# Two-layer hybrid backbone on one core: where the up stage's operands lie, when T3 and T4 are made, and which banks and loads the down stage uses

## Chip, core and metric

One core of one Trainium2 chip runs the whole program. The metric is the device time of one execution in microseconds (us). Engines: TensorE (PE, its weight loads PEld), VectorE (DVE), ScalarE (ACT), GpSimd (POOL), SyncE (SP, here only a queue of DMA issues). Each engine runs its instructions in a fixed order and stops at the first one whose inputs are not there.

## What is computed

A backbone of two layers (DEPTH 2) over 1024 latent tokens and 256 context tokens of width 1024, float32. Cut to what the change touches:

```python
for i in range(2):
    mod_lat = silu(c) @ ada_w[i] + ada_b[i]          # adaLN: shift, scale, gate, twice; six parts of 1024
    mod_ctx = silu(c_ctx) @ ada_w[i] + ada_b[i]
    ...                                               # attention, Hyena, linear attention, output projection
    h_lat = h_lat + g2_l * swiglu(modulate(rms_norm(h_lat, norm2_g), sh2_l, sc2_l), w1, w3, w2)
    if i == 0: h_ctx = h_ctx + g2_c * swiglu(...)     # the context only in the first layer
swiglu(u) = (silu(u @ w1) * (u @ w3)) @ w2            # hidden width 2816 = 22 column blocks of 128
```

## The kernel before

**Products.** A float32 matrix is kept as a rounded high part and a remainder; `split` makes them (ACT casts the high part, POOL subtracts it to get the low part, line 187), and `mm3` multiplies two such operands with three matmuls. A matmul over 512 columns is the unit of work. Weights stand as the stationary operand, tokens as the moving one.

**Up stage** (`up`). Latent tokens are two blocks of 512 (blocks 0 and 1), the context block 2 has 256. Weight column blocks are taken in pairs (p, p+1). Over a pair and the two token blocks the kernel does a block product in Strassen's manner with seven products instead of eight: sums of weight quarters (S1 to S4, DVE, line 1716) against sums of token blocks (T1 to T4, with B11, B21, B22 as the blocks themselves). `norm_sums` is a generator that makes the token sums of block 1 while TensorE works: T1, then B22 and T2, then T3 and T4 (`difference`, lines 1602 and 1603: two DVE subtractions or additions and one on POOL for each quarter, then a cast and a POOL subtraction). Three pairs 0, 2, 4 have their first products (`first`) ahead, while the sums are made; eight whole pairs 6 to 20 follow, and pairs 0, 2, 4 are finished last. In layer 0 `context_tokens()` also normalizes the context block (tile u2, lines 399, 401, 405) before the whole pairs. The split weights go to tiles `hl` (a fixed region) or `hs` (its own tiles, cycled by `ring`). Gated results are written to device memory (`g_d`) by ACT's queue.

**Down stage** (lines 1500 to 1570). For each pair of hidden blocks, `load(j)` brings a block of w2 (`raw`) and of the gated values (`graw`, all 1280 tokens, 1024 in layer 1), splits both into high and low parts (`w2s`, which lies in `hl` or in a tile w2/w; `gs`, tiles g), and TensorE computes 24 outputs (8 output blocks by three token blocks) in turn in the six banks of role 0, (6,7,0,1,2,3). Banks 4 and 5 are role 1. DVE adds each output to the residual h (line 1561), which has to be loaded back from `h_d` in 24 loads (16 in layer 1) at the stage's start.

**adaLN work.** The modulation vectors are computed between the rest of the work, in items of half a part: `ada_dve` has DVE accumulate 8 loaded weight slices (`nsq`, lines 325 to 331) into two tiles `acc`, 16 operations; its `finish` sums them with two matmuls against ones into a bank, ACT copies the row (`nacc`, line 338), four transposes put it into another bank, and DVE adds the bias (line 343). `ada_next()` finishes the last item and begins another. It is called in the output projection, after whole and finishing pairs of `up` in layer 0, and after pairs of the down stage while j < 10.

The order on each engine is set by a list scheduler at build time, from the program's order and a cost model; tiles and banks are reused as their readers finish.

## Time and profile before

| what | value |
| --- | --- |
| time, median of 3 runs | 3799.12 us (3797.28 to 3799.82) |
| profiled execution | 3801.16 us, span 3799.4 us |
| TensorE busy | 3500.2 us, 92% of the span |
| VectorE / ScalarE / GpSimd busy | 2322.3 / 1282.3 / 1801.4 us |
| mean granted TensorE clock | 0.956 |

The span runs from the first to the last instruction; the time has 1.8 us more. TensorE's idle time is the span less its busy time; matmuls that run on one after the other overlap in the rows, so a group's busy time is no sum of its means.

### The profile page before, as it was taken

The numbers are of one execution on the slowest core, as the hardware profiler recorded it, in microseconds if no ns is written. First come the engines' busy times: TensorE is split into PE (matmuls) and PEld (weight loads), VectorE is DVE, ScalarE is ACT, GpSimd is POOL, SyncE is SP. The second block draws the span as 40 slices with busy tenths as digits, with TensorE's granted clock in tenths as the row PEclk, the third lists the DMA queues.
The fourth block names the chain that finished last, engine by engine and source line by source line (L and its number), as shares of the span: only waits on it lengthen the run. The fifth ranks groups of instructions, "written<-read, shape, count | busy, mean of one in ns | idle before, by whom it ended". The sixth has DMA issues, their size and how long they took to land. (4 is left out here: it accounts for less than half of the span.)

```text
span 3799.4 us, 47618 instructions
## 1 busy us (share of the span) xinstructions
PE 3500.2 (92%) x17375; PEld 2617.9 (69%) x17375; DVE 2322.3 (61%) x3569; ACT 1282.3 (34%) x2316; POOL 1801.4 (47%) x1302
## 2 busy tenths in 40 slices
PE   8999899999894999997899799989999888999898
PEld 4789745445673888875678678955544667888787
DVE  6855666863768355585875782668573576435455
ACT  4243243453333333331111323324454343332112
POOL 2424475564346534453323451547764476444442
PEclk9999999899997999998999899989999999999999
DMA  9343311120742233335332234321110632223421
GB/s 322 99 124 118 112 35 55 39 84 21 251 132 75 85 96 106 109 120 170 104 105 93 82 123 135 104 92 50 35 71 26 199 114 73 86 81 112 151 92 67
DMA packets 325450, 394.09 MB, mean 104 GB/s; under 512 B 22999, under 2 KB 227198, under 8 KB 323935
## 3 DMA queue, kind: packets, MB, share of 16 engines
q1 hardware_dynamic: 295583, 332.58, 27.8%
q10 hardware_dynamic: 27072, 44.58, 3.2%
q0 software_dynamic: 2560, 13.89, 1.0%
q8 instruction: 136, 2.23, 0.2%
q14 instruction: 99, 0.81, 0.1%
HBM read 290.57 MB, written 100.40 MB: 103 GB/s over the span
## 5 line engine op out<-in xcount | busy, mean ns | idle before, releaser
L187 POOL TENSOR_TENSOR hl<-raw,hl 128x512 fp32r<-128x512 f32 (+1 forms) x204 | 380.8, 1872 | 550.6 <-ACT hl L423 501.8
L175 PE MATMUL ps<-u,hl 128*128 128x512 f32 (+1 forms) x2640 | 555.5, 363 | 35.7 <-DVE u L405 8.9
L175 PEld LDWEIGHTS ps<-u,hl 128*128 128x128 f32 x2640 | 442.9, 195 | 124.9 <-DVE u L405 12.2
L1561 DVE SCALAR_TENSOR_TENSOR h<-ps,mod,h 128x512 f32<-128x512 f32 (+1 forms) x448 | 301.0, 687 | 230.6 <-PE ps L175 229.2
L175 PE MATMUL ps<-g,hl 128*128 128x512 f32 (+1 forms) x1704 | 386.1, 375 | 51.2 <-ACT g L423 33.7
L1089 POOL TENSOR_TENSOR ac<-ac,p 128x512 f32<-128x512 f32 x256 | 355.5, 1397 | 158.2 <-ACT p L1078 157.2
L175 PEld LDWEIGHTS ps<-g,hl 128*128 128x128 f32 x1704 | 302.7, 195 | 115.7 <-ACT g L423 35.2
L423 ACT CAST hl<-raw 128x512 fp32r<-128x512 f32 (+1 forms) x204 | 162.5, 803 | 484.5 <-PE ps L175 355.7
L175 PE MATMUL ps<-p,V 128*64 128x512 f32 x672 | 312.1, 610 | 3.4 <-DVE sq L1124 2.1
L175 PE MATMUL ps<-T,hs 128*128 128x512 f32 x1056 | 260.8, 400 | 54.7 <-ACT hs L423 44.7
L1053 DVE TENSOR_REDUCE mx<-ps 128x1 f32<-128x512 f32 (+1 forms) x400 | 221.2, 588 | 120.6 <-PE ps L175 119.7
L1078 ACT ACTIVATE p<-ps 128x512 f32<-128x512 f32 (+1 forms) x336 | 194.5, 586 | 286.9 <-PE ps L175 279.2
L331 DVE SCALAR_TENSOR_TENSOR acc<-nsq,silc,acc 128x512 f32<-128x512 f32 x252 | 239.1, 986 | 54.3 <-DMA nsq<-in_ada_w 53.8
L175 PEld LDWEIGHTS ps<-T,hs 128*128 128x128 f32 x1056 | 199.9, 191 | 103.6 <-ACT hs L423 45.5
L175 PEld LDWEIGHTS ps<-Q,K 65*128 65x128 f32 (+1 forms) x672 | 104.5, 190 | 223.3 <-issue 211.2
L175 PE MATMUL ps<-T,hl 128*128 128x512 f32 x1056 | 252.4, 392 | 6.2 <-ACT T L423 3.0
L175 PE MATMUL ps<-g,w 128*128 128x512 f32 (+1 forms) x984 | 233.5, 376 | 11.3 <-DVE mod L343 10.6
L175 PE MATMUL ps<-Q,K 65*128 65x512 f32 (+1 forms) x672 | 241.4, 441 | 1.1 <-ACT p L1078 1.0
L175 PE MATMUL ps<-y,hl 128*128 128x512 f32 (+1 forms) x960 | 215.6, 383 | 22.2 <-ACT hl L423 8.7
L175 PEld LDWEIGHTS ps<-T,hl 128*128 128x128 f32 x1056 | 197.9, 189 | 51.9 <-ACT T L423 3.4
L175 PEld LDWEIGHTS ps<-y,hl 128*128 128x128 f32 x960 | 171.1, 194 | 69.4 <-ACT hl L423 12.1
L175 PEld LDWEIGHTS ps<-g,w 128*128 128x128 f32 x984 | 178.5, 190 | 47.4 <-DVE mod L343 11.5
(318 smaller groups left out, 6162.8 us busy)
## 6 DMA issues: line engine op xcount, KB each, us to landing
raw<-in_ffn_w SPq DMA_DIRECT2D x144, 512.0 KB
nsq<-in_ada_w SPq DMA_DIRECT2D x144, 256.0 KB
g_d<-c ACTq DMA_DIRECT2D x88, 256.0 KB
raw<-in_w_in SPq DMA_DIRECT2D x36, 512.0 KB
raw<-in_w_out SPq DMA_DIRECT2D x32, 512.0 KB
h<-h_d SPq DMA_DIRECT2D x64, 256.0 KB
graw<-g_d SPq DMA_DIRECT2D x22, 640.0 KB
ada<-in_ada_w SPq DMA_DIRECT2D x24, 512.0 KB
```

The lines of the kernel that those rows point to most:

```text
L175: self.nc.tensor.matmul(out, w, x, start=start, stop=stop, **kw)
L187: eng.tensor_tensor(out=out, in0=x, in1=hi.bitcast(F32), op=ALU.subtract)
L331: nc.vector.scalar_tensor_tensor(out=acc[w], in0=raw, scalar=s, in1=acc[w], op0=ALU.mult, op1=ALU.add)
L423: self.nc.scalar.copy(hi, raw)
L1053: nc.vector.tensor_reduce(out=mx[:, j, i:i + 1], in_=pm, op=ALU.max, axis=AX.X)
L1078: nc.scalar.activation(p, st, AF.Exp)
L1089: nc.gpsimd.tensor_tensor(out=acc[j], in0=x, in1=ps[j], op=ALU.add)
L1561: nc.vector.scalar_tensor_tensor(out=h, in0=ps, scalar=self.mod[l][:, 40 + k, w:w + 1], in1=h, op0=ALU.mult, op1=ALU.add)
```

## The change

Five parts. (1) `finish` takes both of its banks from role 1 (banks 4 and 5) wherever it is called; before, in the output projection and the down stage, they came from role 0's cycle. (2) A tile of 64 bytes is put at the head of the pool aux, the tiles of `up` are touched in a fixed order by small POOL memsets, and the down stage's g tiles get fixed names; in the built program all of T, B, u, hl, hs, g and w2 then lie at byte offset 128 modulo 512. Before, T, B, u and hl lay at 128, and hs, g and the tile w at 192. (3) T3 is made after the S4 products of the first whole pair, T4 after that pair's second gated store; before, both were made ahead of `context_tokens()` and of the first whole pair. (4) In the down stage the gated values are loaded and split in two halves (640 or 512 columns), w2 is split ahead of them, and both first loads, j and j+1, are issued before the loads of h; before, only the first was. (5) `ada_next` is not called after the finishing pairs 2 and 4 of `up`, and in the down stage it is called while j < 14.

```diff
@@ -331,12 +331,12 @@
                     nc.vector.scalar_tensor_tensor(out=acc[w], in0=raw, scalar=s, in1=acc[w], op0=ALU.mult, op1=ALU.add)
 
         def finish():
-            ps = self.ps()
+            ps = self.ps(1)
             for w in range(2):
                 self.mm(ps[64 * w:64 * w + 64], self.ones[:, :64], acc[w], True, True)
             rows = self.t(wp, [P, 512], F32, "nacc", 1)[:65]
             nc.scalar.copy(rows, ps[:65])
-            ps = self.ps()[:, :4 * 65].rearrange("p (m r) -> p m r", m=4)
+            ps = self.ps(1)[:, :4 * 65].rearrange("p (m r) -> p m r", m=4)
             for m in range(4):
                 self.tr(ps[:, m], rows[:, m * P:(m + 1) * P], 65)
             out, bias = self.ada_bias(l, part, c0, 4)
@@ -1424,6 +1424,7 @@
         self.open_u0()
         self.auxp = self.pool("aux", 1, side="right", reuse_waits="tile")
         aux = self.aux = self.auxp.__enter__()
+        nc.gpsimd.memset(self.t(aux, [P, 16], F32, "even", 1), 0.0)
         self.hpool = self.pool("h", 1, side="right", reuse_waits="tile")
         hp = self.hpool.__enter__()
         h0c = self.pool("h0", 1, side="right", reuse_waits="tile")
@@ -1521,26 +1522,31 @@
                 raw = self.t((self.wp, wp)[m % 2], [P, KC, P], F32, "raw", 1)
                 nc.sync.dma_start(out=raw.rearrange("p a b -> p (a b)"), in_=A["ffn_w2"][l][m * P:(m + 1) * P, :])
                 i = j % (4 if last else 3)
-                if i < 2:
-                    w2s[m] = self.hl[:, i * 2048:i * 2048 + 2048].rearrange("p (s k c) -> p s k c", s=2, k=KC)
+                x = (0, None, None, 1)[i] if last else (1, None, 0)[i]
+                if x is None:
+                    w2s[m] = self.t(wp, [P, 2, KC, P], F32R, "w2", 2 if last else 1)
                 else:
-                    w2s[m] = self.t(wp, [P, 2, KC, P], F32R, "w2", 2 if last else 1)
-                graw = self.t(gp, [P, nt], F32, "graw", 2 if last else 1)
-                ld = nc.sync.dma_start(out=graw, in_=self.g_d[m][:, :nt])
+                    w2s[m] = self.hl[:, x * 2048:x * 2048 + 2048].rearrange("p (s k c) -> p s k c", s=2, k=KC)
+                self.split(raw, w2s[m][:, 0], w2s[m][:, 1])
+                gs[m] = self.t(gp, [P, 2, nt], F32R, f"g{j % ng}", 1)
+                hn = nt // 2
+                for i in range(2):
+                    graw = self.t(gp, [P, hn], F32, "graw", 4 if last else 3)
+                    ld = nc.sync.dma_start(out=graw, in_=self.g_d[m][:, i * hn:(i + 1) * hn])
+                    self.split(graw, gs[m][:, 0, i * hn:(i + 1) * hn], gs[m][:, 1, i * hn:(i + 1) * hn])
+                return ld
+
+            ng = 4 if last else 3
+            for j in range(0, NHC, 2):
+                p, end = order[j // 2], j == NHC - 2
+                load(j)
+                ld = load(j + 1)
                 if j == 0:
                     with self.tc.issue_after(ld.ins):
                         for b in blks:
                             o, n = BLK[b]
                             for k in range(KC):
                                 nc.sync.dma_start(out=self.h[b][:, k, :], in_=self.h_d[k][:, o:o + n])
-                self.split(raw, w2s[m][:, 0], w2s[m][:, 1])
-                gs[m] = self.t(gp, [P, 2, nt], F32R, "g", 4 if last else 3)
-                self.split(graw, gs[m][:, 0], gs[m][:, 1])
-
-            for j in range(0, NHC, 2):
-                p, end = order[j // 2], j == NHC - 2
-                load(j)
-                load(j + 1)
                 if end and not last:
                     self.n1a = self.norm_scale(l + 1, 1)
                 rngs = [(b, 0, BLK[b][1]) for b in blks]
@@ -1566,7 +1572,7 @@
                         self.finish(b, s, n, r, fp)
                     elif end:
                         norm1 = b, self.spread(r, n, aux)
-                if not last and j < 10:
+                if not last and j < 14:
                     ada_next()
             if norm1:
                 self.norm1(l + 1, *norm1, up)
@@ -1616,8 +1622,10 @@
         yield
         for k in range(4):
             difference("T3", "T2", "B11", k)
+        yield
         for k in range(4):
             difference("T4", "B21", "T2", k)
+        yield
 
     def up(self, l, B, sums, context_tokens, aux, ada_next, nada):
 
@@ -1699,7 +1707,6 @@
             first(p, load(p, (0,)), [{}, {}], i % 2)
             if i < 2:
                 next(sums)
-        next(sums, None)
         if context_tokens:
             uc = context_tokens()
         wpc.__exit__(None, None, None)
@@ -1707,6 +1714,10 @@
         wpc = self.pool("up", 1, side="right", reuse_waits="tile")
         wp = wpc.__enter__()
         extra, ahead, nring = 2 if uc is not None else 5, False, 0
+        places = {n: (k, b) for n, k, b in (("raw", [P, KC, P], 3), ("hs", [P, 2, 4, P], extra), ("c", [P, 512], 6), ("S", [P, 512], 4))}
+        held = [self.t(wp, k, F32R if n == "hs" else F32, n, b) for n, (k, b) in places.items()]
+        for x in held:
+            nc.gpsimd.memset((x if len(x.shape) == 2 else x[:, 0] if len(x.shape) == 3 else x[:, 0, 0])[:, 0:2].bitcast(F32), 0.0)
         order = [*range(len(pre) * 2, NHC, 2), *pre]
         for p in order:
             W = load(p)
@@ -1763,11 +1774,13 @@
                     nc.vector.tensor_tensor(out=s2[w], in0=a[w], in1=m1[w], op=ALU.add)
                 else:
                     nc.scalar.copy(s2[w], a[w])
+            next(sums, None)
             for w in range(2):
                 summed(w, "S4", "A12", "S2", ALU.subtract)
                 product(d[w], parts(W[w]["S4"]), B["B22"], False)
                 nc.vector.tensor_tensor(out=s2[w], in0=d[w], in1=s2[w], op=ALU.add)
             gated(p, 1, s2[0], s2[1])
+            next(sums, None)
             for w in range(2):
                 summed(w, "S3", "A11", "A21", ALU.subtract)
                 product(a[w], parts(W[w]["S3"]), B["T3"], False)
@@ -1797,7 +1810,7 @@
                 for w in range(2):
                     hl[w]["A21"] = parts(W[w]["A21"])
                 context(p + 1, "A21", "A22")
-            if nada and p != order[0]:
+            if nada and p != order[0] and p not in pre[1:]:
                 ada_next()
         wpc.__exit__(None, None, None)
         return order```

The 64-byte tile is the diff's line with "even". What the scheduler makes of it, at three places:

SyncE's queue in layer 0, at the end of the pairs done ahead and the start of the first whole pair; before (s are products of the three pairs that were parked in `m_d`, raw the first whole pair's weights, nsq adaLN weights):

```order
L1673 DMA raw_10706<-in_ffn_w 128x8x128 [waits DMAHW1_49,Pool_49]
L325 DMA nsq_11470<-in_ada_w 128x512 [waits DMAHW2_49,DVE_49,PE_49]
L325 DMA nsq_11474<-in_ada_w 128x512 [waits DMAHW6_49,DMAHW4_49,PE_49]
L1726 DMA s_14026<-m_d_46_114 128x512 [waits DMAHW5_49,DMAHW6_49,DVE_49,Pool_49]
L1726 DMA s_14027<-m_d_46_114 128x512 [waits DMAHW6_49,DMAHW0_49,DVE_49]
L1673 DMA raw_10708<-in_ffn_w 128x8x128 [waits DMAHW7_49]
L1673 DMA raw_10710<-in_ffn_w 128x8x128 [waits DMAHW3_49,DMAHW1_49,DMAHW0_49]
L1673 DMA raw_10712<-in_ffn_w 128x8x128 [waits DMAHW3_49]
```

The same place in the changed kernel:

```order
L1681 DMA raw_10660<-in_ffn_w 128x8x128 [waits DMAHW0_49,Pool_49]
L325 DMA nsq_11480<-in_ada_w 128x512 [waits DMAHW2_49,DVE_49,PE_49]
L325 DMA nsq_11484<-in_ada_w 128x512 [waits DMAHW6_49,DMAHW4_49,PE_49]
L1681 DMA raw_10662<-in_ffn_w 128x8x128 [waits DMAHW3_49,DMAHW5_49,DMAHW1_49,DMAHW6_49,DVE_49,Activation_49]
L1681 DMA raw_10664<-in_ffn_w 128x8x128 [waits DMAHW7_49,DMAHW0_49]
L1681 DMA raw_10666<-in_ffn_w 128x8x128 [waits Pool_49]
L1737 DMA s_14036<-m_d_46_114 128x512 [waits DVE_49,DMAHW2_49,Activation_49,Pool_49]
L1737 DMA s_14037<-m_d_46_114 128x512 [waits DVE_49,DMAHW4_49,Activation_49,Pool_49]
```

The three weight loads stood behind the two loads of s, and now stand ahead of them. In both kernels the s loads wait for DVE and POOL work of this place.

VectorE in the down stage of layer 0, where one adaLN item ends and the next begins (L1561 and L1567 add an output to h; L343 frees the bank of the transposes); before, at the end of a pair:

```order
L1561 SCALAR_TENSOR_TENSOR h_2913_15150<-ps_15639,mod_11_79,h_2913_15150 128x256 [waits PE_49]
L329 TENSOR_SCALAR acc_15658<-nsq_15660,silc_66 128x512 [waits DMAHW0_49,PE_49]
L329 TENSOR_SCALAR acc_15659<-nsq_15660,silc_66 128x512 [waits DVE_49,PE_49]
L331 SCALAR_TENSOR_TENSOR acc_15658<-nsq_15664,silc_66,acc_15658 128x512 [waits DMAHW1_49,DVE_49]
L331 SCALAR_TENSOR_TENSOR acc_15659<-nsq_15664,silc_66,acc_15659 128x512 [waits DVE_49]
L331 SCALAR_TENSOR_TENSOR acc_15658<-nsq_15668,silc_66,acc_15658 128x512 [waits DMAHW2_49,DVE_49]
L331 SCALAR_TENSOR_TENSOR acc_15659<-nsq_15668,silc_66,acc_15659 128x512 [waits DVE_49]
L343 TENSOR_TENSOR mod_12_80<-ps_15652,vecs_76 128x8 [waits PE_49]
L331 SCALAR_TENSOR_TENSOR acc_15658<-nsq_15672,silc_66,acc_15658 128x512 [waits DMAHW3_49,DVE_49]
L331 SCALAR_TENSOR_TENSOR acc_15659<-nsq_15672,silc_66,acc_15659 128x512 [waits DVE_49]
L1561 SCALAR_TENSOR_TENSOR h_2911_15148<-ps_15711,mod_11_79,h_2911_15148 128x512 [waits PE_49]
```

In the changed kernel:

```order
L1567 SCALAR_TENSOR_TENSOR h_2892_15070<-ps_15543,mod_11_79,h_2892_15070 128x256 [waits PE_49]
L1567 SCALAR_TENSOR_TENSOR h_2892_15070<-ps_15551,mod_11_79,h_2892_15070 128x256 [waits PE_49]
L343 TENSOR_TENSOR mod_12_80<-ps_15852,vecs_76 128x8 [waits PE_49]
L331 SCALAR_TENSOR_TENSOR acc_15858<-nsq_15884,silc_66,acc_15858 128x512 [waits DMAHW5_49,DVE_49]
L1567 SCALAR_TENSOR_TENSOR h_2892_15070<-ps_15559,mod_11_79,h_2892_15070 128x256 [waits PE_49]
L1567 SCALAR_TENSOR_TENSOR h_2892_15070<-ps_15567,mod_11_79,h_2892_15070 128x256 [waits PE_49]
L331 SCALAR_TENSOR_TENSOR acc_15859<-nsq_15884,silc_66,acc_15859 128x512 [waits DVE_49]
L1567 SCALAR_TENSOR_TENSOR h_2892_15070<-ps_15575,mod_11_79,h_2892_15070 128x256 [waits PE_49]
L331 SCALAR_TENSOR_TENSOR acc_15858<-nsq_15888,silc_66,acc_15858 128x512 [waits DMAHW6_49,DVE_49]
L331 SCALAR_TENSOR_TENSOR acc_15859<-nsq_15888,silc_66,acc_15859 128x512 [waits DVE_49]
L329 TENSOR_SCALAR acc_16122<-nsq_16124,silc_66 128x512 [waits DMAHW7_49,PE_49]
```

Before, six accumulations stand in a block between two pairs, with L343 behind them; now accumulations and additions to h alternate, and L343 stands among the additions.

TensorE at the start of the down stage of layer 0 (T4 products are the last of the up stage); before:

```order
L175 MATMUL ps_14779<-T_2287_10231,hl_5951 128x512 x9
L184 MATMUL ps_15100<-shapes_64,nacc_15098 128x65 [waits Activation_49]
L184 MATMUL ps_15100<-shapes_64,nacc_15098 128x65 x3
L175 MATMUL ps_15199<-g_15187,hl_5951 128x512 [waits DVE_49,Activation_49]
L175 MATMUL ps_15207<-g_15187,hl_5951 128x512
```

In the changed kernel:

```order
L175 MATMUL ps_14744<-T_2288_10233,hl_5951 128x512 x9
L184 MATMUL ps_15325<-shapes_64,nacc_15323 128x65 [waits Activation_49]
L184 MATMUL ps_15325<-shapes_64,nacc_15323 128x65 x3
L175 MATMUL ps_15583<-acc_15331,ones_67 64x512 [waits DVE_49,PE_49]
L175 MATMUL ps_15583<-acc_15332,ones_67 64x512 [waits DVE_49]
L175 MATMUL ps_15128<-g_2896_15081,hl_5951 128x512 [waits Activation_49]
L175 MATMUL ps_15136<-g_2896_15081,hl_5951 128x512
```

The sums of a further adaLN item (acc against ones) now stand ahead of the stage's first product; before, they stood behind the whole first pair.

## Rows read from the trace of the kernel before

**Rows 1.** The page, part 1: busy us (share of the span) x instructions, by engine.

```profile
PE 3500.2 (92%) x17375; PEld 2617.9 (69%) x17375; DVE 2322.3 (61%) x3569; ACT 1282.3 (34%) x2316; POOL 1801.4 (47%) x1302
```

**Rows 2.** Windows: from:to length, busy us (x instructions) by engine, clock, DMA.

```profile
1166.00:1247.00 81.00, 38.50 (x165) 30.80 (x166) 64.16 (x66) 26.31 (x49) 58.66 (x43) 0.73 0.27 78
3099.00:3164.00 65.00, 51.33 (x192) 39.15 (x192) 62.82 (x43) 22.13 (x39) 63.11 (x39) 0.89 0.18 53
1755.00:1792.00 37.00, 12.67 (x34) 8.75 (x33) 12.85 (x16) 4.61 (x4) 13.22 (x5) 0.63 0.85 294
1816.00:1852.00 36.00, 30.69 (x154) 25.14 (x152) 32.36 (x41) 4.73 (x6) 10.81 (x5) 0.95 0.39 124
3514.00:3534.00 20.00, 8.97 (x25) 5.99 (x24) 1.39 (x2) 4.57 (x5) 6.63 (x3) 0.72 0.82 293
```

**Rows 3.** Groups of TensorE by form: count | busy us, mean ns | idle before.

```profile
L175 PE MATMUL ps<-g,hl 128*128 128x512 f32 x1248 | 322.0, 409 | 49.2 <-ACT g L423 33.7 <-DVE mod L343 10.6 <-POOL g L187 4.7
...
L175 PE MATMUL ps<-T,hs 128*128 128x512 f32 x1056 | 260.8, 400 | 54.7 <-ACT hs L423 44.7 <-ACT c L1689 7.5 <-ACT c L1765 1.6
...
L175 PE MATMUL ps<-u,hs 128*128 128x512 f32 x360 | 91.5, 405 | 4.8 <-ACT c L1786 4.8
...
L175 PE MATMUL ps<-B,hs 128*128 128x512 f32 x168 | 40.5, 395 | 0.0
```

**Rows 4.** Timeline of TensorE: start us, duration us, what, [idle before <-releaser].

```profile
1737.26 5.60 PE L175 MATMUL ps<-B,hl 128*128 128x512 f32 x24
...
1742.70 5.76 PE L175 MATMUL ps<-T,hs 128*128 128x512 f32 x24
...
1816.00 3.01 PE L175 MATMUL ps<-g,w 128*128 128x512 f32 x12
...
1963.77 3.03 PE L175 MATMUL ps<-g,hl 128*128 128x512 f32 x12
```

**Rows 5.** Timeline of SyncE and TensorE, first layer, end of the sums.

```profile
1201.59 2.52 SPq L1673 DMA_DIRECT2D raw<-in_ffn_w  x3
...
1207.27 1.22 PE L175 MATMUL ps<-T,hs 128*128 128x512 f32 x2 [40.44 <-ACT hs L423]
...
1243.80 2.91 PE L175 MATMUL ps<-T,hl 128*128 128x512 f32 x12
```

**Rows 6.** Timeline of VectorE and TensorE, down stage of the first layer.

```profile
1816.10 5.51 DVE L329 TENSOR_SCALAR acc<-nsq,silc 128x512 f32<-128x512 f32 x2 [0.52 <-PE ps L175]
...
1826.48 1.65 PE L175 MATMUL ps<-g,w 128*128 128x512 f32 x3 [5.31 <-DVE mod L343]
...
1936.74 1.65 PE L175 MATMUL ps<-g,w 128*128 128x512 f32 x3 [5.29 <-DVE mod L343]
```

**Rows 7.** Groups of VectorE by form, 1827 to 1863 us, the same pair.

```profile
L331 DVE SCALAR_TENSOR_TENSOR acc<-nsq,silc,acc 128x512 f32<-128x512 f32 x14 | 12.9, 946 | 1.4 <-DMA nsq<-in_ada_w 1.4
...
L1561 DVE SCALAR_TENSOR_TENSOR h<-ps,mod,h 128x512 f32<-128x512 f32 x16 | 11.4, 742 | 0.3 <-PE ps L175 0.2
```

**Rows 8.** Timeline of TensorE, last whole pair of the up stage, first layer.

```profile
1715.21 3.14 PE L175 MATMUL ps<-u,hs 128*128 128x256 f32 x13 [4.11 <-DVE mod L343]
```

**Rows 9.** Timeline of SyncE, VectorE and TensorE, start of down, first layer.

```profile
1763.95 15.46 SPq L1535 DMA_DIRECT2D h<-h_d  x24
...
1764.55 4.39 DVE L331 SCALAR_TENSOR_TENSOR acc<-nsq,silc,acc 128x512 f32<-128x512 f32 x4 [1.59 <-DMA nsq<-in_ada_w]
...
1769.67 7.12 PE L175 MATMUL ps<-g,hl 128*128 128x512 f32 x18 [14.27 <-ACT g L423]
...
1786.28 2.93 PE L175 MATMUL ps<-g,hl 128*128 128x512 f32 x6 [9.49 <-ACT g L423]
```

**Rows 10.** Timeline of TensorE, start of the down stage, second layer.

```profile
3519.04 2.76 PE L175 MATMUL ps<-g,hl 128*128 128x512 f32 x6 [4.05 <-ACT g L423]
...
3533.29 2.93 PE L175 MATMUL ps<-g,hl 128*128 128x512 f32 x6 [5.93 <-ACT g L423]
```

**Rows 11.** Waits of TensorE, 1963 to 2112 us: us in total, times, longest.

```profile
PE ps L175 <- POOL g L187: 2.7, 4, 0.7
```

## What the change does to the time: the prediction

> **What bounds the kernel now.** I read the page's busy times first: TensorE works for 3500.2 us of a span of 3799.4 [rows 1], so 299 us are left in which it stands, and nothing else comes near it over the whole. What a change can bring is therefore a hole in TensorE's work that closes, or a matmul that takes less time. Next I cut the stretches that the change touches into windows [rows 2]. Two kinds of holes show. From 1166 to 1247 us, where T3, T4 and the context are made and the first whole pair runs, TensorE is busy for 38.5 of 81 us, while DVE works 64.2 and POOL 58.7. At 1755 and at 3514 us, where the down stage starts, nobody works much (DVE 12.9 of 37 us) and the DMA share is 0.85: a stage that waits for loads. A third kind lies within the down stage: in the 36 us of a pair with adaLN work TensorE is busy 30.7 us and DVE 32.4. Then I read the timelines at these places for the wait that ends last.
>
> The profiled execution took 3801.2 us, 1.8 more than its span and 2.0 more than the median of the three runs; the sum below is made against 3801.2, and 2.0 are taken off at the end. A difference of 0.2%, 7.6 us, is about what a measurement of this kernel can tell from none.
>
> **Offsets modulo 512.** The operands of one product, matmul by matmul at full clock: 24 products of B with hl take 5.60 us, 24 of T with hs 5.76 [rows 4]; 12 of g with w take 3.01, 12 of g with hl 3.03. In the built program the pairs that differ in offset (128 against 192) are T,hs, B,hs, u,hs and g,hl; those that share one are B,hl and g,w. So the row's difference is 0.16/24 = 6.7 ns a matmul for the first three forms, of which there are 1056 + 360 + 168 = 1584 of 512 columns [rows 3], or 10.6 us, and 0.02/12 = 1.7 ns for 1248 of g,hl, or 2.1 us. Together 12.7 us; some of them lie where TensorE waits for others anyway (48 of T,hs in the first whole pair of each layer, the g,hl of four pairs), so I take 10, with 0 and 13 as ends. The narrow products of 256 columns I leave unpriced. The lower end holds if the difference belongs to hs for another reason than its address. The Trainium skill speaks for that end: "SBUF — State Buffer", section "Who interferes with whom", gives TensorE two SBUF read ports that are independent, one for the moving operand and one for weight loads, and no rule that ties them by address; by it the sum would be 10 us less. The rows, where two forms of equal shape differ, bear out that something does; that it is the address no run shows yet.
>
> **T3 and T4 later, layer 0.** TensorE's hole of 40.4 us ends at 1207.3, and the three weight loads for the products behind it went out at 1201.6 [rows 5], behind the loads of s, which waited for DVE and POOL to be done with sums and context. In the changed queue they stand ahead. The hole shrinks to the context's own normalization and the loads, but the sums are not gone: their 16 DVE and 16 POOL pairs of operations now compete with the weight sums and splits of the first whole pair, ahead of the T3 and T4 products in it. Up to the last T4 product (1243.8 + 2.9) the stretch is 81 us with DVE 64.2 and POOL 58.7 [rows 2]. Layer 1 has no context to wait for and shows what it looks like when sums and pair are mixed: 65 us with DVE 62.8 and POOL 63.1 busy and TensorE 51.3. If DVE's work fills the new stretch as well as it fills that one, it takes 66 us, a gain of 15; if the pair takes layer 1's 65 us after some 12 us of context and loads before its first product (an estimate: 5.7 us lie between loads and first product in [rows 5], and the context's operations were mixed with the sums before), 77 us, a gain of 4; and if nothing packs better, 0. I take 8, with 0 and 15. For layer 1 itself, where the sums are mixed with the pair already, 0.
>
> **adaLN banks and the later calls in the down stage.** In a pair with adaLN work TensorE comes to the bank that holds the transposes and waits 5.3 us for L343, which stands on DVE behind six accumulations, two of which alone take 5.51 [rows 6]; this repeats in four pairs (first at 1826.5, last at 1936.7), which take 1963.8 - 1816.0 = 147.8 us [rows 4], 36.9 each. With own banks that wait has no place. What remains late is DVE: it is busy 32.4 of 36 us in such a pair [rows 2]. If it becomes the bound at this load, each pair gains 36.9 - 32.4 = 4.5 at most; the order has 71 accumulations in the four pairs that follow the first, not 64, as the first calls moved out of `up`, which at 0.95 each [rows 7] takes 7 us back: 18 - 7 = 11. If alternating with the additions, instead of starting in a block beside POOL's splits, makes accumulations cheaper, TensorE is the bound: its 30.7 busy us of such a pair [rows 2] instead of 36.9, a gain of 4 x 6.2 = 25. If DVE also keeps its short waits for nsq (1.4 us a pair [rows 7]) and loses the overlap, 3. I take 15.
>
> **The last adaLN call of `up`.** Two items leave the finishing pairs. The wait before the first of them belongs to the call that stays; the one in the last finishing pair, 4.1 us behind L343 [rows 8], goes: 4, with 2 and 5 as ends. The two `finish` move to the down stage, so that their matmuls cost what they did.
>
> **Start of the down stage, layer 0.** Before, TensorE waits 14.3 us for the first g and 9.5 for the second member's [rows 9]: the second loads stand behind 24 loads of h, which take SyncE 15.5 us from 1763.95 on. In the changed code both members' loads go ahead of h. But the queue still holds the last two nsq loads before them, each waiting for an accumulation, and TensorE has the sums of a further adaLN item ahead of its first product. That item's last accumulations ended at 1764.55 + 4.39 = 1768.9 before, 14 us after the last T4 product, and delayed nobody; now TensorE waits for them. Four of its sixteen accumulations stand earlier now, and the w2 load between its loads stays, so I put their end 10 us after T4 and the first product at 11.5: 3 better than 14.5. The second member's loads are then issued before the first product, and of its 9.5 + 0.5 I leave 1. Together 12, with 5 (the accumulations end as late as before, and half of the second wait stays) and 17 as ends.
>
> **Start of the down stage, layer 1.** Waits of 4.05 and 5.93 us [rows 10], by the same two causes, without adaLN work. Half a g is cast and split ahead of the rest, but ACT and POOL have two w2 splits to do before the second member: I take 3 of the 10, ends 0 and 7.
>
> **Halves within the loop.** In pairs without adaLN work TensorE waits for POOL's split of g, four times and 2.7 us in all from 1963 to 2112 us [rows 11]; halves should remove most: 2, ends 0 and 3. More DMAs (44 for 22) are covered by pairs of 29 us. In the output projection own banks change no wait that I could find in the order: the products there wait for ACT's row and DVE's sums before and after: 0.
>
> **Sum.** 10 + 8 + 15 + 4 + 12 + 3 + 2 = 54. 3801.2 - 54 = 3747.2, and 2.0 less for the median: 3745.
>
> **Rivals.**
> First, DVE and POOL stay the bound, so that T3 and T4 give 0 and the adaLN pairs 3: 10 + 0 + 3 + 4 + 12 + 3 + 2 = 34, 3765. For it speaks that both are at 97% in layer 1's mixed stretch [rows 2], and that two first accumulations take 5.5 us beside a POOL split [rows 6] where a later one takes 0.95. Against it, that DVE has a third of its time free in the pairs around. The Trainium skill has the mechanism: in the same section, a DVE instruction with two SBUF inputs and a GpSimd one that reads SBUF exclude each other for a whole instruction; the trace agrees as far as the durations just named go. Chance 0.20.
> Second, the offsets mean nothing (above): 44, 3755. Chance 0.12.
> Third, TensorE is the bound all over: 13 + 15 + 25 + 5 + 17 + 7 + 3 = 85, 3714. For it speaks that a later accumulation takes 0.95 us on the mean, not far from an addition's 0.74 [rows 7]; against it that POOL works 10.8 of 36 us [rows 2] and will lie beside some of them wherever they stand. Chance 0.10.
> Fourth, slower than before. Each accumulation of the spread items waits for its nsq load, and the additions to h stand behind it on DVE; the nsq loads stand on SyncE behind halves of g that wait for POOL to free a buffer. If each of the 40 loads of the five items came late past what six banks hide, TensorE would stop 40 times. It decides when a load is more than 1.4 + 0.2 us late each time, since 54 + 8 us have to be lost; now the wait is 1.4 us in a whole pair of eight loads [rows 7]. At 2 us each: 80 - 54 = 26 us slower, 3825. Chance 0.05.
> Fifth, no difference, with the parts' gains at their lower ends and some of the fourth: 0.03.
>
> **How the numbers follow.** My own forecast has the remaining 0.50: 54 us, 3745. Its neighbours on the long side (3755, 3765) and on the short side (3714) lie within gains of 24 to 84, which I take as the range, 3715 to 3775 (from 3799): it leaves out the slower case, the equal one, the rest of the third and some of the first, some 2 in 10. All cases but the last two are faster by more than 0.2%: 0.92; within 0.2%: 0.03; slower: 0.05.
>
> **What would show it.** Offsets right: 24 of T with hs in 5.60 us and 12 of g with hl in 3.01; wrong: 5.76 still. T3 and T4: the hole after 1166 us ends before 1185, and the last T4 product of the first whole pair comes about 70 to 75 us after it began, with waits for POOL's T splits ahead of T3; wrong, if the stretch keeps 81 us. adaLN pairs: no wait of TensorE for L343, and a period of 30 to 34 us; if the period stays at 36, DVE is busy throughout. Down stage: first product 11 to 12 us after T4, preceded by the acc sums, second wait under 3 us. The prediction is wrong above all if DVE's accumulations take longer where they now stand, since two of the larger terms rest on them.

## The result

The changed kernel takes 3732.69 us, the median of four runs (3723.03 to 3742.72), against 3798.20 (3788.87 to 3799.82): a ratio of 0.9833, 95% interval 0.9802 to 0.9863. It is faster, by 65.5 us; 53 were forecast (3745, range 3715 to 3775). The profiled execution took 3731.27, with a span of 3729.5, 69.9 less than before.

Cut at products of TensorE in the two traces (at the end of the context's norm sums, elsewhere at the start of the product named), the 69.9 us lie here. Times are in us, a pair is a pair of hidden blocks, T4 products are those with the sum T4, and the last 11 us of the span, nearly the same in both, are left out:

| stage | before | after | gain |
|---|---|---|---|
| program start to the context's norm sums | 1166.8 | 1164.1 | 2.7 |
| from there to the last T4 product of the first whole pair, layer 0 | 79.5 | 67.6 | 11.9 |
| rest of up, layer 0 | 508.5 | 499.2 | 9.3 |
| last T4 product to the second down pair, layer 0 | 61.2 | 45.3 | 15.9 |
| second to fifth pair | 147.8 | 141.4 | 6.4 |
| sixth to last pair | 172.7 | 168.4 | 4.3 |
| layer 1 up to its whole pairs | 963.0 | 957.2 | 5.8 |
| first whole pair, layer 1 | 64.2 | 64.0 | 0.2 |
| rest of up, layer 1 | 350.9 | 345.2 | 5.7 |
| last T4 product to the second down pair, layer 1 | 38.8 | 31.8 | 7.0 |
| the other pairs | 234.9 | 234.5 | 0.4 |

The first row and the seventh hold next to no edited code (the banks of four adaLN finishes in the first, 24 products with hs in each), and 8.5 us of the gain lie in them. In the runs below the first whole pair starts between 1173 and 1192 us where nothing ahead of it differs, and the seventh row goes from 957 to 980. A second profile of the changed kernel (the timed run below) has 960.9 in the seventh row and every other row within 0.8 us of the table; two profiles of the kernel with pinned sums, below, agree within 1.7. So the stages are compared one by one and not by totals, and a difference of 1 or 2 us in a stage tells little.

The page after, busy time of each engine [rows 1]:

```profile
PE 3473.7 (93%) x17375; PEld 2606.3 (70%) x17375; DVE 2316.0 (62%) x3569; ACT 1285.9 (34%) x2360; POOL 1810.1 (49%) x1356
```

Windows of after (busy time of PE, PEld, DVE, ACT and POOL, granted clock, DMA): the first whole pair of layer 0, the second to the fourth down pair, and a pair without adaLN work [rows 2]:

```profile
1164.00:1232.00 68.00, 44.22 (x194) 35.79 (x194) 60.81 (x55) 26.72 (x50) 62.59 (x48) 0.82 0.22 64
1776.00:1813.00 37.00, 31.83 (x155) 25.68 (x155) 35.60 (x48) 5.44 (x8) 13.19 (x6) 0.91 0.45 138
1813.00:1848.00 35.00, 32.13 (x155) 25.56 (x154) 34.36 (x46) 5.13 (x8) 13.06 (x6) 0.95 0.44 140
1848.00:1881.00 33.00, 33.00 (x158) 24.84 (x157) 30.81 (x47) 5.62 (x9) 12.57 (x6) 1.00 0.48 145
...
2002.00:2029.50 27.50, 27.50 (x146) 23.73 (x145) 15.26 (x25) 4.45 (x7) 10.87 (x6) 1.00 0.28 86
```

In the first, POOL is now busy for 62.6 of 68 us and DVE for 60.8, much as in layer 1 before: they are near the bound there. In the adaLN pairs DVE is nearly full in some (35.6 of 37) and less so in others (30.8 of 33).

The timeline of TensorE after, in the first whole pair: the hole of [rows 5] went from 40.44 to 16.16, and two short waits took part of its place.

```profile
1180.25 1.22 PE L175 MATMUL ps<-T,hs 128*128 128x512 f32 x2 [16.16 <-ACT hs L423]
...
1201.84 3.06 PE L175 MATMUL ps<-T,hl 128*128 128x512 f32 x12 [3.62 <-ACT c L1697]
...
1219.09 2.17 PE L175 MATMUL ps<-T,hl 128*128 128x512 f32 x7 [3.08 <-DVE c L1787]
```

The timeline after at the start of the down stage of layer 0 [rows 9]: the loads of h now follow those of both members, TensorE stands 12.90 us for the accumulations of a further adaLN item, and the second member's wait of 9.49 is gone.

```profile
1742.01 3.19 SPq L325 DMA_DIRECT2D nsq<-in_ada_w  x2
1744.33 2.54 PE L175 MATMUL ps<-acc,ones 128*64 128x512 f32 x4 [12.90 <-DVE acc L331]
1746.57 0.33 SPq L1535 DMA_DIRECT2D graw<-g_d  x1
1746.79 2.92 PE L175 MATMUL ps<-g,hl 128*128 128x512 f32 x6
1746.95 14.69 SPq L1549 DMA_DIRECT2D h<-h_d  x24
```

The waits of TensorE from the second to the fifth down pair, before and after (us in total, times, longest):

```profile
PE ps L175 <- DVE mod L343: 21.2, 4, 5.3
```

```profile
PE ps L175 <- DVE h L1567: 12.5, 4, 4.9
```

No wait for L343 is left [rows 6, 7], but in its place TensorE waits for the additions to h. In the second pair five accumulations stand in one block on DVE beside POOL's splits and take 11.14 us, 2.2 each, and TensorE waits 4.87 us for the additions behind them:

```profile
1776.96 3.01 POOL L187 TENSOR_TENSOR hl<-raw,hl 128x1024 fp32r<-128x1024 f32 x1 [7.96 <-ACT hl L423]
...
1778.01 11.14 DVE L331 SCALAR_TENSOR_TENSOR acc<-nsq,silc,acc 128x512 f32<-128x512 f32 x5
...
1789.87 7.65 PE L175 MATMUL ps<-g,hl 128*128 128x512 f32 x24 [4.87 <-DVE h L1567]
```

The 24 matmuls behind that wait took 7.65 us; 24 of the same form took 5.63 at 1776.06, before it. Windows over wait and recovery show that TensorE's granted clock (a share of full speed; its two levels are 1.2 and 2.4 GHz) fell to the lower level for a part of them (a mean of 0.77, then 0.73) and came back. So this wait cost about 2 us more than its length:

```profile
1784.00:1789.80 5.80, 1.00 (x5) 0.50 (x3) 5.80 (x5) 0.72 (x1) 5.32 (x3) 0.77 0.52 174
1789.80:1797.50 7.70, 7.63 (x26) 5.87 (x26) 6.70 (x11) 0.00 (x0) 0.82 (x1) 0.73 0.68 221
1797.50:1806.00 8.50, 8.50 (x38) 6.41 (x38) 8.10 (x13) 0.59 (x1) 0.00 (x0) 1.00 0.33 94
```

### The profile page after: what moved, and what is told of

Its sections match the earlier page's. It is cut to its first block, busy times and chain, and to the rows that moved or that the text cites. A ratio compares the mean times of both kernels' runs of the same rounds, so it can differ in the third digit from the quotient of the medians.

```text
span 3729.5 us, 47823 instructions
## 1 busy us (share of the span) xinstructions
PE 3473.7 (93%) x17375; PEld 2606.3 (70%) x17375; DVE 2316.0 (62%) x3569; ACT 1285.9 (34%) x2360; POOL 1810.1 (49%) x1356
## 5 line engine op out<-in xcount | busy, mean ns | idle before, releaser
L187 POOL TENSOR_TENSOR hl<-raw,hl 128x512 fp32r<-128x512 f32 (+1 forms) x203 | 377.6, 1865 | 527.1 <-ACT hl L423 474.3
L175 PE MATMUL ps<-u,hl 128*128 128x512 f32 (+1 forms) x2640 | 548.3, 360 | 38.0 <-ACT hl L423 18.9
L175 PEld LDWEIGHTS ps<-u,hl 128*128 128x128 f32 x2640 | 436.7, 192 | 124.8 <-ACT hl L423 20.9
L1567 DVE SCALAR_TENSOR_TENSOR h<-ps,mod,h 128x512 f32<-128x512 f32 (+1 forms) x448 | 300.5, 687 | 189.4 <-PE ps L175 188.3
L175 PE MATMUL ps<-g,hl 128*128 128x512 f32 (+1 forms) x1632 | 390.9, 370 | 13.6 <-DVE h L1567 9.7
L175 PEld LDWEIGHTS ps<-g,hl 128*128 128x128 f32 x1632 | 288.9, 192 | 73.0 <-DVE h L1567 13.2
L175 PE MATMUL ps<-p,V 128*64 128x512 f32 x672 | 311.2, 609 | 4.0 <-DVE sq L1124 2.8
L423 ACT CAST hl<-raw 128x512 fp32r<-128x512 f32 (+1 forms) x203 | 161.2, 801 | 401.3 <-PE ps L175 300.4
L175 PE MATMUL ps<-T,hs 128*128 128x512 f32 x1056 | 254.8, 395 | 28.5 <-ACT hs L423 19.9
L331 DVE SCALAR_TENSOR_TENSOR acc<-nsq,silc,acc 128x512 f32<-128x512 f32 x252 | 247.6, 1016 | 47.7 <-DMA nsq<-in_ada_w 47.1
L175 PE MATMUL ps<-g,w 128*128 128x512 f32 (+1 forms) x1056 | 270.8, 371 | 5.9 <-POOL g L187 2.9
L175 PE MATMUL ps<-T,hl 128*128 128x512 f32 x1056 | 254.6, 394 | 14.7 <-DVE c L1787 5.8
L175 PEld LDWEIGHTS ps<-Q,K 65*128 65x128 f32 (+1 forms) x672 | 104.6, 190 | 222.5 <-issue 210.4
L175 PEld LDWEIGHTS ps<-T,hs 128*128 128x128 f32 x1056 | 200.2, 191 | 72.4 <-ACT hs L423 20.7
L175 PE MATMUL ps<-Q,K 65*128 65x512 f32 (+1 forms) x672 | 241.8, 441 | 1.2 <-ACT p L1078 1.1
L175 PEld LDWEIGHTS ps<-T,hl 128*128 128x128 f32 x1056 | 198.6, 190 | 59.6 <-DVE c L1787 4.1
L175 PE MATMUL ps<-y,hl 128*128 128x512 f32 (+1 forms) x960 | 217.3, 385 | 22.2 <-ACT hl L423 8.9
L175 PEld LDWEIGHTS ps<-y,hl 128*128 128x128 f32 x960 | 172.2, 196 | 69.5 <-ACT hl L423 12.9
L175 PEld LDWEIGHTS ps<-g,w 128*128 128x128 f32 x1056 | 190.2, 190 | 41.4 <-DVE h L1567 3.4
```

The source lines that it names most:

```text
L175: self.nc.tensor.matmul(out, w, x, start=start, stop=stop, **kw)
L187: eng.tensor_tensor(out=out, in0=x, in1=hi.bitcast(F32), op=ALU.subtract)
L331: nc.vector.scalar_tensor_tensor(out=acc[w], in0=raw, scalar=s, in1=acc[w], op0=ALU.mult, op1=ALU.add)
L423: self.nc.scalar.copy(hi, raw)
L1567: nc.vector.scalar_tensor_tensor(out=h, in0=ps, scalar=self.mod[l][:, 40 + k, w:w + 1], in1=h, op0=ALU.mult, op1=ALU.add)
```

## Experiments

Theories at the start: each part gives its own gain, the offsets by address, the down stage by the order of its loads and by banks; against them, that DVE and POOL are the bound in the adaLN pairs, and that the offsets mean nothing. Each kernel is the changed one with the edit shown, and executed once unless a number of runs is given; "up" and "down" without a layer are those of layer 0, and "down" runs from the last T4 product to the last product of the stage.

**Offsets.** The tile that shifts the operands is left out, so that hs, g and w start at 192 modulo 512 again while T, B and u stay at 128; or, in a second kernel, it is half as long (`[P, 8]`), and they start at 160. The first one's edit:

```diff
-        nc.gpsimd.memset(self.t(aux, [P, 16], F32, "even", 1), 0.0)
```

> Only the 64-byte tile at the head of aux is taken out of the changed kernel: hs, g and the tile w go back to byte 192 modulo 512, T, B, u and hl stay at 128, and the instructions are the same. If the address makes the difference, 24 products of T with hs take 5.75 to 5.77 us again (5.6 in the changed kernel), those of B with hl stay at 5.60, and the program takes 10 to 13 us more than the changed one (about 3743 against its profiled 3731). If something else in the change made hs faster (the fixed order of its tiles), T with hs stays at 5.60 and the time at 3731, within 8.

> The tile has 32 bytes instead of 64: hs, g and w at 160, the others at 128. If any difference within 512 bytes costs the same, T with hs takes 5.75 us for 24; if the cost grows with the distance, about 5.68; if only multiples of 64 bytes count, 5.60. The time is between 3731 and 3745.

Timeline of the two kernels and of the changed one, 24 products of T with hs in the last pair of up:

```profile
1715.55 5.76 PE L175 MATMUL ps<-T,hs 128*128 128x512 f32 x24
```

```profile
1710.89 5.75 PE L175 MATMUL ps<-T,hs 128*128 128x512 f32 x24
1716.48 5.61 PE L175 MATMUL ps<-T,hl 128*128 128x512 f32 x24
```

```profile
1718.89 5.60 PE L175 MATMUL ps<-T,hs 128*128 128x512 f32 x24
```

With 64 or 32 bytes between the offsets T,hs takes 5.76 and 5.75, with one offset 5.60, and T,hl, which always shares one, 5.61. It is the address. 18 products of g with hl in a down pair, in the changed kernel, at 192 and at 160:

```profile
2005.83 4.24 PE L175 MATMUL ps<-g,hl 128*128 128x512 f32 x18
```

```profile
2002.48 4.28 PE L175 MATMUL ps<-g,hl 128*128 128x512 f32 x18
```

```profile
2014.16 4.36 PE L175 MATMUL ps<-g,hl 128*128 128x512 f32 x18
```

Here, where the moving operand g is the shifted one, the distance counts: 64 bytes cost 2 ns a matmul, 32 bytes 7. That the offsets count modulo 512 no run shows; only 128, 160 and 192 were tried.

At 192 the rest of up takes 503.7 us against 499.2, that of layer 1 348.4 against 345.2, and its first whole pair and the down pairs 1.2 more: 8.9 us in all. At 160 the rest of up takes 500.8, only 1.6 more. The kernels below whose up is that of the changed one lie between 497.6 and 499.9 there, so 8.9 is good to some 2 us. The totals (3736.31 at 192, 3751.98 at 160) say less: the first is 5.0 above the changed kernel's profile, where 10 to 13 were expected.

**T3 and T4.** The sums go back ahead of the context.

```diff
             if i < 2:
                 next(sums)
+        next(sums, None)
+        next(sums, None)
...
-            next(sums, None)
...
-            next(sums, None)
```

> T3 and T4 are made ahead of the context and of the first whole pair again, all else as changed. If their place makes the gain, the stretch from the context's norm sums on TensorE to the end of the first pair's T4 products takes 79 us in layer 0 again instead of 67.5, with a hole of 40 us in it, and the program some 12 us more (3743). If the hole's end was set by the loads of the first whole pair alone, the stretch stays at 67 to 70. Layer 1 the same in either case (64 us).

Timeline of this kernel, TensorE:

```profile
1174.38 0.70 PE L175 MATMUL ps<-nsq,ones 128*128 128x256 f32 x2 [1.51 <-DVE s L1592]
1217.73 1.22 PE L175 MATMUL ps<-T,hs 128*128 128x512 f32 x2 [42.65 <-ACT hs L423]
```

The hole is back, and from norm sums to T4 it takes 81.2 us against 67.6: 13.6. In layer 1 the first whole pair keeps its time (63.9). Total 3763.18: of the 32 us more, 21.5 lie in the first and the seventh row.

**Banks.** The adaLN finish takes the shared banks again.

```diff
-            ps = self.ps(1)
+            ps = self.ps()
...
-            ps = self.ps(1)[:, :4 * 65].rearrange("p (m r) -> p m r", m=4)
+            ps = self.ps()[:, :4 * 65].rearrange("p (m r) -> p m r", m=4)
```

> finish takes its banks from role 0's cycle again, all else as changed. If own banks free the adaLN pairs of the down stage from the wait for the line that adds the bias, the four pairs behind the first take 147 us again instead of 141 and TensorE waits for that line in each; the program takes 5 to 12 us more. If DVE alone sets these pairs, they keep 141 within 2 us.

Waits of TensorE in the second to seventh pair (us in total, times, longest), and its timeline at the start of down:

```profile
PE ps L175 <- DVE mod L343: 25.5, 6, 4.3
```

```profile
1732.53 6.71 PE L175 MATMUL ps<-g,hl 128*128 128x512 f32 x18 [8.52 <-ACT g L423]
1762.62 1.08 PE L175 MATMUL ps<-acc,ones 128*64 128x512 f32 x4
```

The waits for L343 are back, now in six pairs of 35.1 to 36.4 us, and down takes 366.9 us against 355.1. The expectation was put on the second to the fifth pair alone, and there it failed: they take 143.0 us, not 147, which is its rival's case (141 within 2). The loss stands in the sixth and seventh pair, 71.7 us against 56.7. In the traces each of the second to seventh pairs holds 16 accumulations here, while the changed kernel has done all of its accumulations by the end of the fifth pair, 72 of them in the second to the fifth. And the start is 5 us quicker: the sums stand within the first pair here, at 1762.62, and the first product comes 8.5 us after the last T4 product and not 15.6. So own banks, which should only remove a wait, also let the adaLN work be placed earlier, and its sums ahead of the first product, where TensorE waits for them. Total 3736.33.

**Loads of h, calls, and the place of the sums.** Four kernels on one chip.

h stands behind the first member's loads only; the second member is loaded behind h:

```diff
-                load(j)
-                ld = load(j + 1)
+                ld = load(j)
...
+                load(j + 1)
```

> The 24 loads of h stand ahead of the second member's loads again; all else is as in the change. If SyncE's queue is what held the second member before the change, its wait comes back in the first pair of the down stage: 6 to 10 us between the two members, the time from the last T4 product to the second pair goes from 45.1 to 51 to 55 us, and the run is 6 to 9 us longer than the changed kernel's. Rival: the second wait went because the first product now starts later, behind the adaLN sums, and the loads of h are covered by that; then the time to the second pair stays at 45 to 46 us.

```profile
1738.81 16.13 SPq L1548 DMA_DIRECT2D h<-h_d  x24
...
1761.26 2.93 PE L175 MATMUL ps<-g,w 128*128 128x512 f32 x6 [10.27 <-ACT g L423]
```

The wait of TensorE for the second member is back, at 10.27 us behind 16.13 of issues on SyncE (timeline), and from T4 to the second pair it takes 63.0 us against 45.3, more than expected: with 2.2 us of smaller waits 12.5 us are waits, and the products themselves take 5.9 us longer, at a granted clock of 0.56 in the 9 us behind the long wait. In layer 1 it takes 41.7 against 31.8. Total 3760.52.

The two calls go back into up, and leave down:

```diff
-                if not last and j < 14:
+                if not last and j < 10:
...
-            if nada and p != order[0] and p not in pre[1:]:
+            if nada and p != order[0]:
```

> The two adaLN calls stand in the finishing pairs of up again, and five calls instead of seven in the down stage; banks, offsets and the rest are as in the change. If an item costs DVE time wherever it stands, the four adaLN pairs of the down stage get shorter (141.4 us to 132 to 137), and up gets some 4 us longer or less, since its waits for the adaLN sums were those of shared banks: the run is 0 to 6 us shorter than the changed kernel's. Rival, as the prediction had it: the call in the last finishing pair costs 4 us wherever its banks are, and the down stage's pairs stay at 140 us or more: 4 us longer.

```profile
1703.63 5.49 PE L175 MATMUL ps<-u,hs 128*128 128x256 f32 x24 [3.12 <-DVE mod L343]
```

The last finishing pair's wait is back although the finish has own banks: in up these are also the banks of the narrow products. (The wait in the finishing pair ahead of it, 5.6 us, belongs to the call that stays and is there in both kernels.) The rest of up takes 507.2 us against 499.2, down 344.6 against 355.1 (second to fifth pair 132.9). So moving the calls gained 8.0 in up and lost 10.5 in down: by itself it loses some 2.5, not much more than such sums are good to. (Total 3752.88, with 23 us more than after in the seventh row.)

The sums are pinned: they may not be placed ahead of the first product of their pair; `one` is the last matmul of it, and every TensorE instruction of the call comes behind it:

```diff
+                        if b == blks[0] and k == 0:
+                            one = self.mmi
...
-                    ada_next()
+                    with self.tc.issue_after(one.ins):
+                        ada_next()
```

> The matmuls of the adaLN sums in the down stage may not be placed ahead of the first product of the pair in which they are called; all else is as in the change. If the sums of a further item set the start of the down stage, the first product comes 9 to 10 us after the last T4 product instead of 15.6, the time to the second pair goes from 45.1 to 39 to 41 us, and the run is 4 to 6 us shorter than the changed kernel's. Rival: the loads of w2 and g set the start; then it stays at 15 us and the run is as long.

Timeline of TensorE, then windows of the third and fourth pair:

```profile
1737.70 6.47 PE L175 MATMUL ps<-g,hl 128*128 128x512 f32 x18 [8.61 <-ACT g L423]
...
1748.18 1.08 PE L175 MATMUL ps<-acc,ones 128*64 128x512 f32 x4
```

```profile
1802.80:1833.60 30.80, 29.50 (x154) 24.06 (x153) 26.82 (x44) 5.00 (x8) 11.29 (x6) 1.00 0.46 150
1833.60:1862.80 29.20, 29.20 (x155) 24.27 (x153) 25.20 (x44) 5.24 (x8) 10.90 (x6) 1.00 0.51 156
```

The start is shorter as expected (first product 8.6 us after the last T4 product, 40.9 to the second pair). What was not expected is the next four pairs: 122.5 us instead of 141.4. TensorE is busy throughout or nearly so, at full clock, and its waits there, 12.5 us in the changed kernel, come to 2.9:

```profile
PE ps L175 <- DVE h L1569: 1.9, 2, 1.3
PE ps L175 <- DVE acc L331: 1.0, 1, 1.0
```

3.4 us of the gain are given back in the sixth to last pair, where some of the adaLN work now stands; down takes 335.1 us against 355.1. The order of TensorE's instructions shows why (here at the start of down, - the changed kernel, + this one):

```
 L175 MATMUL ps_14744<-T_2288_10233,hl_5951 128x512 x12
-L184 MATMUL ps_15325<-shapes_64,nacc_15323 128x65 x4
-L175 MATMUL ps_15583<-acc_15331,ones_67 64x512
-L175 MATMUL ps_15583<-acc_15332,ones_67 64x512
 L175 MATMUL ps_15128<-g_2896_15081,hl_5951 128x512
...
+L175 MATMUL ps_15583<-acc_15331,ones_67 64x512
+L175 MATMUL ps_15583<-acc_15332,ones_67 64x512
 L175 MATMUL ps_15439<-g_2942_15369,hl_5951 128x512 x3
```

The sums of acc_15331, which are called in the second pair (the products with g_2942), stood ahead of the first product of the first pair; so it goes on from pair to pair, and with the sums the accumulations stood ahead of the additions. The groups of DVE over these pairs, of the changed kernel, of this one and (accumulations only) of the next:

```profile
L331 DVE SCALAR_TENSOR_TENSOR acc<-nsq,silc,acc 128x512 f32<-128x512 f32 x64 | 70.9, 1128 | 0.1
```

```profile
L331 DVE SCALAR_TENSOR_TENSOR acc<-nsq,silc,acc 128x512 f32<-128x512 f32 x61 | 52.4, 886 | 2.8 <-DMA nsq<-in_ada_w 2.8
```

```profile
L332 DVE SCALAR_TENSOR_TENSOR ps<-nsq,silc,ps 128x512 f32<-128x512 f32 x48 | 34.3, 750 | 9.0 <-DMA nsq<-in_ada_w 8.8
```

An accumulation takes 886 ns on the mean here and 1128 in the changed kernel. It isn't the block as such. Set against POOL's operations in the traces, 22 of the 64 in the changed kernel overlap one in time and take 1.87 us on the mean, and the other 42 take 0.74; with the pin 9 of 61 overlap one (1.71 us) and 52 do not (0.74). So fewer of them meet POOL's splits when they stand between the additions. The last row is the fourth kernel: pin, and the running sums held in the two PSUM banks, so that DVE reads one SBUF operand.

```diff
+        run = [self.ps(1) for w in range(2)] if banked else acc
...
-                    nc.vector.scalar_tensor_tensor(out=acc[w], in0=raw, scalar=s, in1=acc[w], op0=ALU.mult, op1=ALU.add)
+                    nc.vector.scalar_tensor_tensor(out=(run if k < KC - 1 else acc)[w], in0=raw, scalar=s, in1=run[w], op0=ALU.mult, op1=ALU.add)
```

> As the run with the sums pinned, and in the down stage the adaLN accumulations are held in the two banks of their own (the last one writes SBUF), so that DVE reads one SBUF operand and not two. If DVE is held beside POOL's splits by its second SBUF operand, the first accumulations of a pair take under 1.2 us instead of 2.2 each, the mean one falls from 0.95 to about 0.75 us, and the four adaLN pairs take 122 to 132 us instead of 141.4: 10 to 18 us less than with the pin alone. Rival: nsq loads or TensorE set these pairs; then they stay at 138 to 142 us, with TensorE or the loads as the releaser.

Each accumulation falls to 0.75 us, as expected, the same for the 28 that overlap a POOL operation and the 28 that do not. The four pairs fall to 120.9, 1.6 less than with the pin alone and not 10 to 18. So DVE's accumulations with two SBUF operands are slowed beside POOL, but with the sums in their place that no longer holds TensorE. Totals 3723.01 (pin) and 3709.27 (pin and PSUM). With the pin alone the unedited part ahead of layer 1's whole pairs took 973.1 us against 957.2, behind one wait:

```profile
2290.11 2.29 PE L175 MATMUL ps<-tm,u 128*128 128x288 f32 x8 [15.44 <-ACT tm L423]
```

**Halves, and timed runs.** One load and one split a block of g, with one buffer (layer 1: two):

```diff
-                hn = nt // 2
-                for i in range(2):
-                    graw = self.t(gp, [P, hn], F32, "graw", 4 if last else 3)
+                hn = nt
+                for i in range(1):
+                    graw = self.t(gp, [P, hn], F32, "graw", 2 if last else 1)
```

> The gated values are loaded and split in one piece of 1280 (1024) columns with one (two) buffers, as before the change; all else is as in the change. If halves are what shortened the pairs without adaLN work and the start of the second layer's down stage, the pairs from the sixth on go from 27.5 back to 28.2 to 28.6 us, and the time from the last T4 product to the second pair in layer 1 goes from 31.8 to 34 to 37: 6 to 10 us longer in the down stages than the changed kernel. Rival, as the prediction sized it: 2 us in the pairs and 3 at the start in all. If the loads ahead of h alone did it, nothing changes.

TensorE, sixth to last pair: waits of this kernel; of the changed one there are none.

```profile
PE ps L175 <- POOL g L187: 3.3, 5, 0.7
```

T4 to the second pair takes 51.6 us against 45.3, the second to fifth pair 2.6 more, the others 4.8 more: 13.7 in layer 0. Layer 1 loses 0.6 at the start and gains 2.3 behind it. Total 3760.02.

The changed kernel again, the pinned one, and pin and PSUM sums with no call in any finishing pair (`p not in pre`, `j < 16`):

> The changed kernel itself, for comparison on this chip: 3720 to 3740 us.

> The run with the pinned sums once more, timed. The down stage of layer 0 took 335.1 us from the last T4 product to its end, against 355.1 in the changed kernel. If only the placing of the sums differs, the whole is 20 us shorter, 3713; in its first profile 16 us of this were lost between the down stage and layer 1's up stage, in code that wasn't edited, behind one wait of 15.4 us for the cast of tm. If that belongs to the order in which the program was laid out, and not to chance, it is there again and the time is 3718 to 3727.

> Pinned sums, accumulations in the two banks, and no adaLN call in any of the three finishing pairs of up: one more call in the down stage. If a call costs about 4 us in a finishing pair, up is 4 to 9 us shorter than with the call (the waits of 2.7 and 5.75 us in the first finishing pair go), and one more pair of the down stage takes 30.2 us instead of 27.5: 2 to 6 us shorter in these two stages than the run with pin and banks, whose profile took 3709. Rival: the waits in that pair belong to its narrow products, not to the call; then up stays as it is and the run is 2 to 3 us longer.

| kernel | median us | runs | ratio to before, 95% |
|---|---|---|---|
| changed | 3734.40 | 5 | 0.9841 (0.9825 to 0.9857) |
| sums pinned | 3728.30 | 4 | 0.9830 (0.9812 to 0.9848) |
| pinned, PSUM sums, no calls in finishing pairs | 3710.52 | 4 | 0.9790 (0.9769 to 0.9811) |

The pinned kernel keeps its 20 us in down (334.8) and loses 12 of them again to the other part (972.6, with a wait of 15.5 us for tm once more): the wait belongs to the order in which this program came out, not to chance. Its interval overlaps that of the changed kernel, so the whole program isn't shown to be faster for the pin alone. The last one is the best of the three: the rest of up takes 488.4 us, 10.2 less than with the call (pin and PSUM sums: 498.6), down 337.0, 2.8 more. It is 24 us faster than the changed kernel, and their runs just don't overlap (up to 3725.32, from 3725.84). Against the kernel with pin and PSUM sums, whose one execution took 3709.27, its total shows no gain.

## Why the prediction was right, and where it was off

The time came out 12 us below the forecast. That it lies so near is in part luck: one large term was 8.6 too high, four others were too low by 2 to 4 each, and 8.5 us lie in two rows for which next to nothing was forecast. Term by term, predicted and measured:

- **Offsets: 10, measured 8.9** (good to some 2). Right, and by address, as the kernels at 192 and 160 show. The Trainium skill ("SBUF — State Buffer", section "Who interferes with whom") has two independent read ports for TensorE and no rule by address; here the measurement decides: 5.76 against 5.60 us for 24 products.
- **T3 and T4, layer 0: 8, measured 11.9** (13.6 when undone). Of the two ways in which the prediction bounded it, the packing of layer 1 was the nearer: 67.6 us, where 66 and 77 were named. For layer 1, 0 was right (0.2).
- **adaLN pairs: 15, measured 6.4.** The term that failed. "With own banks that wait has no place" held: 21.2 us of waits for L343 are gone. But the term worked out the length of a pair from busy times, with accumulations and additions in turn, and its 15 left no room for a wait of TensorE for the additions. In fact own banks also freed the finish to be placed ahead of its pair, the accumulations went ahead in blocks, and TensorE stood 12.5 us for the additions behind them. The accumulations as a whole did not become dearer, which the prediction named as its main danger: with the first ones (L329, 2800 ns each before and 1035 after) 64 of them took 73.7 us before and 72 take 79.0 now. Their place did it, as the pin shows: own banks alone give pairs of 33.0 to 36.8 us, the sums in their own pair on shared banks 35.1 to 36.4, and both together 29.2 to 33.2. The 25 us of the prediction's upper end, where TensorE is the bound, are what both give (147.8 - 122.5 = 25.3, of which 3.4 come back as cost in later pairs). The first rival (DVE and POOL as the bound) described these pairs better than the forecast, but not its cause: with the pin alone, accumulations at 886 ns no longer hold TensorE. The Trainium skill's rule of the same section, that a DVE instruction with two SBUF inputs contends with a GpSimd one that reads SBUF, agrees with the traces: such accumulations take 1.7 to 2.0 us on the mean beside a POOL operation and 0.74 without, and 0.75 in both cases with one input in PSUM. The first accumulations, which the prediction took as evidence for that rule, are another case: L329 reads one tile from SBUF. Before, all 8 of them overlapped a POOL operation and took 2.8 us each; now the 4 that overlap none take 0.48. Once the sums were pinned, putting the second input into PSUM was worth 1.6 us in these pairs.
- **The last call of up: 4, measured 4.8** (9.3 for the rest of up less 4.5 for offsets). The wait of [rows 8], which lies in the last finishing pair and not in a whole one, is gone. When the calls were put back, it was 8.0; why the two differ by 3 isn't settled. The prediction counted the accumulations that moved to down within the term for the pairs, but there they cost 10.5, more than up gains.
- **Start of down, layer 0: 12, measured 15.9.** The sum is near, its parts are not. The first product was to come 3 us earlier, at 11.5 after the last T4 product; it came at 15.6, 1.1 later than before, because TensorE waits for the adaLN sums. The second wait went altogether (10.0 us, where 9 were counted), and the order of the loads of h is worth 17.7 when undone. The other 7.0 us had no term: TensorE is busy for 29.2 us in this pair where it was for 36.3, and the mean granted clock, 0.66 to 0.71 in the first 30 us of that pair before, is 0.86 in the first 10 and 1.00 in the rest now.
- **Start of down, layer 1: 3, measured 7.0.** Mis-sized: the loads of h alone are worth 9.9 there, the halves 0.6. The prediction had ACT and POOL bound the second member; SyncE's queue did.
- **Halves: 2, measured 4.3** over the sixth to the last pair, which includes 1.6 lost by the moved calls (166.8 us with the calls back, against 168.4). Undone they cost 13.7 us in layer 0, most of it outside these pairs, where the prediction gave them nothing.

The stages with edited code add up to 61.1 us where 54 were forecast; another 8.5 us of the profiled difference lie in the two rows with next to no edited code. The fourth rival, late nsq loads behind halves of g, did not appear: accumulations in the second to fifth pair wait 0.1 us in all. Two things were not undone by themselves, and their share lies in the terms above: that w2 is split ahead of the gated values, and that the weight loads of the first whole pair go out ahead of the loads of s.

## What to carry to other kernels

A resource of its own removes a wait and also an ordering: look in the built order where the freed work goes, and pin it if it moves ahead of inputs that aren't ready. In the down stage that was worth more than the resource (20 us against 12), and it was seen only by cutting the trace stage by stage, since unedited stages moved by as much. Count work that is moved at what it costs where it lands: two calls saved 8 us in one stage and cost 10.5 in the next; with the pin and the sums in PSUM another call saved 10.2 and cost 2.8. And price a wait by its length and by what the clock takes behind it: 7 of the 16 us at the start of down came from that.

## What the runs showed of the hardware

With the stationary operand (hs) at byte 192 or 160 and the moving one (T) at 128, modulo 512, a matmul of 512 columns took 6 to 7 ns longer than with both at 128 (24 in 5.76 and 5.75 us against 5.60). With the moving operand (g) shifted and the stationary one (hl) at 128 it took 2 ns longer at 192 and 7 at 160 (18 in 4.28 and 4.36 us against 4.24).

A DVE accumulation (SCALAR_TENSOR_TENSOR, 128x512, f32) with two operands in SBUF took 0.74 us when no POOL operation overlapped it and 1.7 to 2.0 on the mean when one did; with one of them in PSUM it took 0.75 either way.

A wait of 4.87 us was followed by 24 matmuls in 7.65 instead of 5.63 us, at a mean granted clock of 0.73.
